# ReLU and row sum of 64 MiB on one core: row blocks laid out contiguously, and one store of short runs in place of one store of long runs

## The chip, the cores and the metric

The kernel runs on one core of one Trainium2 chip. The metric is the device time of an execution in microseconds (us). The span of a profile is mostly about 1.3 us shorter than that time.

## The reference

```python
x = np.random.randn(32, 512, 1024).astype(np.float32)     # 64 MiB
def reference(x):
    return np.sum(np.maximum(x, 0), axis=-1)               # (32, 512), 64 KiB
```

There are 16,384 rows of 4 KiB, and each gives one number.

## The kernel before

The rows are spread over 128 partitions, 128 rows for each. The first region gives every partition 112 consecutive rows. It is loaded in seven transfers of 16 rows per partition (8 MiB). The second region gives every partition 16 rows. It is loaded in ever smaller pieces (8, 4, 2, 1 rows, then the last row in three parts), so that little work is left after the last byte. All loads go through the SyncE queue, into three buffers.

```python
REGIONS = [112, 16]
CHUNKS = [(0, 0), (0, 16), (0, 32), (0, 48), (0, 64), (0, 80), (0, 96)]
...
xv = [xr[P * s : P * (s + n), :].rearrange("(p j) d -> p j d", p=P)
      for s, n in zip(start, REGIONS)]
ov = [of[P * s : P * (s + n)].rearrange("(p j) -> p j", p=P) ...]
...
for c in range(NBIG + 1):
    if c >= NB:
        sp.wait_ge(s_dve, done[c - NB])          # the buffer is free again
    if c < NBIG:
        g, j = CHUNKS[c]
        sp.dma_start(out=buf[:, c % NB, :, :], in_=xv[g][:, j : j + BIG, :]).then_inc(s_in[c], 16)
...                                              # the pieces of the last region
sp.wait_ge(s_fact, 1); sp.wait_ge(s_fdve, 1)     # the seven blocks are reduced
for g in range(len(REGIONS) - 1):                # runs once: 128 runs of 112 x 4 = 448 B
    sp.dma_start(out=ov[g][:, :], in_=res[:, start[g] : start[g] + REGIONS[g]]).then_inc(s_store, 16)
...                                              # ScalarE and VectorE work
sp.wait_ge(s_tdve, 1)                            # the last row is reduced
sp.dma_start(out=ov[-1][:, :], in_=res[:, start[-1] : J]).then_inc(s_out, 16)
sp.wait_ge(s_store, 16 * (len(REGIONS) - 1))
sp.wait_ge(s_out, 16)
```

In six of the blocks ScalarE applies ReLU and VectorE sums the rows. The other rows are done whole by one engine or the other. The change does not touch this.

Of the kernel before, what the change touches and what calls it, by code (L numbers as in the profile page):

```python
# [3 lines left out]
P = 128  # L4
D = 1024
BIG = 16
NB = 3
REGIONS = [112, 16]
CHUNKS = [(0, 0), (0, 16), (0, 32), (0, 48), (0, 64), (0, 80), (0, 96)]
ACT_STEPS = [[7, 9], [7, 9], [4, 5, 7], [4, 5, 7], [4, 5, 7], [3, 4, 5]]  # L10
DVE_STEPS = [[7, 9], [7, 4, 5], [4, 5, 7], [4, 5, 7], [4, 5, 7], [3, 4, 5]]
TAIL = [8, 4, 2, 1]
LAST = [512, 256, 256]


def bass_relu_sum_kernel(
# [15 lines left out]

    B, S, _ = x.shape
    J = B * S // P
    NBIG = len(CHUNKS)
    assert BIG * NBIG + sum(TAIL) + 1 == J == sum(REGIONS) and sum(LAST) == D

    xr = x.rearrange("b s d -> (b s) d")
    of = out.rearrange("b s -> (b s)")
    start = [sum(REGIONS[:i]) for i in range(len(REGIONS))]  # L40
    xv = [
        xr[P * s : P * (s + n), :].rearrange("(p j) d -> p j d", p=P)
        for s, n in zip(start, REGIONS)
    ]
    ov = [of[P * s : P * (s + n)].rearrange("(p j) -> p j", p=P) for s, n in zip(start, REGIONS)]

    buf = nc.alloc_sbuf_tensor("buf", [P, NB, BIG, D], fp32)
    last = nc.alloc_sbuf_tensor("last", [P, LAST[2] + 2], fp32)
    half = nc.alloc_sbuf_tensor("half", [P, 2], fp32)
    res = nc.alloc_sbuf_tensor("res", [P, J], fp32)  # L50

    n_in = NBIG + len(TAIL) + len(LAST)
    s_in = [nc.alloc_semaphore(f"s_in{i}") for i in range(n_in)]
# [7 lines left out]
    s_store = nc.alloc_semaphore("s_store")  # L61
    s_out = nc.alloc_semaphore("s_out")

    sp, act, dve = nc.sync, nc.scalar, nc.vector
# [4 lines left out]

    tb = NBIG % NB  # L70

# [6 lines left out]
    )  # L78
    for c in range(NBIG + 1):
        if c >= NB:  # L80
            sp.wait_ge(s_dve, done[c - NB])
        if c < NBIG:
            g, j = CHUNKS[c]
            sp.dma_start(out=buf[:, c % NB, :, :], in_=xv[g][:, j : j + BIG, :]).then_inc(
                s_in[c], 16
            )
        if c == 0:
            code.insert(arrival, code.pop())
    r = 0
    tail = []  # L90
    for i, n in enumerate(TAIL):
        sp.dma_start(out=buf[:, tb, r : r + n, :], in_=xv[-1][:, r : r + n, :]).then_inc(  # L92
            s_in[NBIG + i], 16
        )
# [7 lines left out]
        )  # L102
    sp.wait_ge(s_fact, 1)
    sp.wait_ge(s_fdve, 1)
    for g in range(len(REGIONS) - 1):
        sp.dma_start(
            out=ov[g][:, :], in_=res[:, start[g] : start[g] + REGIONS[g]]
        ).then_inc(s_store, 16)


    def on_act(t, acc):
# [11 lines left out]
    for c in range(NTWO):  # L123
# [17 lines left out]
        for n in DVE_STEPS[c]:  # L141
            if ready[r + n - 1] > seen:
# [3 lines left out]
                out=res[:, c * BIG + r : c * BIG + r + n],  # L146
                in_=buf[:, c % NB, r : r + n, :],
# [14 lines left out]
    for r, n, s in tail[:-1]:  # L162
# [6 lines left out]
    r, _, s = tail[-1]  # L169
# [6 lines left out]
        out=res[:, j0 + r : j0 + r + 1], in0=half[:, 0:1], in1=half[:, 1:2], op=ALU.add  # L176
    )

    n = LAST[2]
# [7 lines left out]


    sp.wait_ge(s_tdve, 1)
    sp.dma_start(out=ov[-1][:, :], in_=res[:, start[-1] : J]).then_inc(s_out, 16)  # L190
    sp.wait_ge(s_store, 16 * (len(REGIONS) - 1))
    sp.wait_ge(s_out, 16)


# [26 lines left out]
```

## Time and profile before

| | before |
|---|---|
| time, median | 161.12 us (161.08 to 161.19, 3 runs) |
| span of the profile | 159.8 us |
| DMA queue occupied | 98.0% |
| a block of 8 MiB lands every | 19.35 us |
| large store: issue to landing | 10.7 us, at 157.96 us |
| small store: issue to landing | 1.4 us, at 159.7 us |

The rows are in the prediction below. For a kernel that waits for data, the instructions that open each block are a clock: their starts mark the landings, and their differences are the service times of the DMA engines.

### The profile page before, as it was taken

The numbers are of one execution on the slowest core, as the hardware profiler recorded it, in microseconds if no ns is written. First come the engines' busy times: TensorE is split into PE (matmuls) and PEld (weight loads), VectorE is DVE, ScalarE is ACT, GpSimd is POOL, SyncE is SP. The second block draws the span as 40 slices with busy tenths as digits, with TensorE's granted clock in tenths as the row PEclk, the third lists the DMA queues.
The fourth block names the chain that finished last, engine by engine and source line by source line (L and its number), as shares of the span: only waits on it lengthen the run. The fifth ranks groups of instructions, "written<-read, shape, count | busy, mean of one in ns | idle before, by whom it ended". The sixth has DMA issues, their size and how long they took to land.

```text
span 159.8 us, 148 instructions
## 1 busy us (share of the span) xinstructions
DVE 121.4 (76%) x58; ACT 101.5 (63%) x55; POOL 0.2 (0%) x4
## 2 busy tenths in 40 slices
DVE  0000000999959999999969989699899999598995
ACT  3000059990699808996099951999339980496974
POOL 0000000000000000000000000000000000000000
DMA  7996996996997998989969969969969969899994
GB/s 262 525 525 262 525 525 262 525 525 262 525 443 344 525 410 377 525 361 427 525 295 492 525 279 509 525 262 525 525 262 525 525 262 525 353 435 394 406 393 138
DMA packets 2305, 67.18 MB, mean 420 GB/s; under 512 B 512, under 2 KB 768, under 8 KB 1024
## 3 DMA queue, kind: packets, MB, share of 16 engines
q1 hardware_dynamic: 2304, 67.18, 98.0%
q14 instruction: 1, 0.01, 0.0%
HBM read 67.11 MB, written 0.07 MB: 420 GB/s over the span
## 4 chain that ended last, share of the span: by engine, by line
DMA 68%; ACT 18%; DVE 11%; SPq 1%; issue 0%
DMA buf<-in_x_dram 68%; ACT buf L130 18%; DVE res L145 11%; SPq L92 1%; SPq L100 0%; DVE buf L115 0%; DVE last L115 0%
## 5 line engine op out<-in xcount | busy, mean ns | idle before, releaser
L145 DVE TENSOR_REDUCE res<-buf 128x7 f32<-128x7168 f32 (+4 forms) x17 | 100.1, 5923 | 34.0 <-ACT buf L130 34.0
L130 ACT ACTIVATE buf<-buf 128x7168 f32<-128x7168 f32 (+4 forms) x16 | 80.7, 5099 | 46.5 <-DMA buf<-in_x_dram 46.5
L112 ACT ACTIVATE buf<-buf 128x1024 f32<-128x1024 f32 (+1 forms) x19 | 19.0, 1000 | 9.0 <-DMA buf<-in_x_dram 8.9
L115 DVE TENSOR_SCALAR_CACHE_REDUCE buf<-buf 128x1024 f32<-128x1024 f32 (+2 forms) x19 | 20.9, 1146 | 2.8 <-DMA buf<-in_x_dram 2.5
L112 ACT ACTIVATION_READ_ACCUMULATOR buf<-buf 128x1 f32 x19 | 3.5, 186 | 0.0
L130 ACT ACT_TABLE_LOAD x1 | 1.3, 1283 | 0.8 <-PEq L206 0.8
L115 DVE DVE_READ_ACCUMULATOR buf<-buf 128x1 f32 x19 | 1.6, 83 | 0.0
L115 DVE TENSOR_SCALAR_CACHE_REDUCE last<-last 128x258 f32<-128x258 f32 x1 | 0.4, 422 | 0.0
L175 DVE TENSOR_TENSOR res<-half 128x1 f32<-128x1 f32 x1 | 0.2, 160 | 0.1
L206 POOL MEMSET const-bfloat16-1.0<- 128x1 bf16 x1 | 0.1, 101 | 0.0
L206 POOL MEMSET const-uint8-127<- 128x1 uint8 x1 | 0.1, 101 | 0.0
L206 POOL MEMSET const-float32-0.0<- 128x1 f32 x1 | 0.1, 98 | 0.2 <-issue 0.2
L206 POOL MEMSET const-float32-1.0<- 128x1 f32 x1 | 0.1, 98 | 0.0
L115 DVE DVE_READ_ACCUMULATOR last<-last 128x1 f32 x1 | 0.1, 81 | 0.0
## 6 DMA issues: line engine op xcount, KB each, us to landing
buf<-in_x_dram SPq DMA_DIRECT2D x1, 4096.0 KB, 26.7
buf<-in_x_dram SPq DMA_DIRECT2D x1, 2048.0 KB, 31.2
buf<-in_x_dram SPq DMA_DIRECT2D x1, 1024.0 KB, 33.2
buf<-in_x_dram SPq DMA_DIRECT2D x1, 512.0 KB, 34.0
buf<-in_x_dram SPq DMA_DIRECT2D x1, 256.0 KB, 34.2
buf<-in_x_dram SPq DMA_DIRECT2D x1, 128.0 KB, 34.1
last<-in_x_dram SPq DMA_DIRECT2D x1, 128.0 KB, 34.0
buf<-in_x_dram SPq DMA_DIRECT2D x7, 36.3
```

The lines of the kernel that those rows point to most:

```text
L92: sp.dma_start(out=buf[:, tb, r : r + n, :], in_=xv[-1][:, r : r + n, :]).then_inc(s_in[NBIG + i], 16)
L112: return act.activation(t, t, AF.Relu, accum_out=acc)
L115: return dve.tensor_scalar(out=t, in0=t, scalar1=0.0, scalar2=None, op0=ALU.max, op1=ALU.add, accum_out=acc)
L130: act.activation(t, t, AF.Relu).then_inc(s_act, 1)
L145: dve.tensor_reduce(out=res[:, c * BIG + r : c * BIG + r + n], in_=buf[:, c % NB, r : r + n, :], axis=X, op=ALU.add,).then_inc(s_dve, 1)
L175: dve.tensor_tensor(out=res[:, j0 + r : j0 + r + 1], in0=half[:, 0:1], in1=half[:, 1:2], op=ALU.add)
L206: nc = _bacc.Bacc("TRN2", target_bir_lowering=False, num_devices=1)
```

## The change

Each of the seven blocks becomes 2,048 consecutive rows, contiguous in memory. A partition's 16 rows then stand 64 KiB after its neighbour's, where they stood 448 KiB apart. The loads become simpler in form. In return, the results of a partition for the seven blocks lie 8 KiB apart in the output, so one store writes 896 runs of 64 B in place of 128 runs of 448 B.

```diff
-REGIONS = [112, 16]
-CHUNKS = [(0, 0), (0, 16), (0, 32), (0, 48), (0, 64), (0, 80), (0, 96)]
+NREG = 8
...
+    xr = x.rearrange("b s d -> (b s) d").rearrange("(g p j) d -> g p j d", g=NREG, p=P)
+    xv = [xr[g] for g in range(NREG)]
+    bulk = of[0 : P * BIG * NBIG].rearrange("(g p j) -> p g j", p=P, j=BIG)
+    tail_out = of[P * BIG * NBIG :].rearrange("(p j) -> p j", p=P)
...
-            g, j = CHUNKS[c]
-            sp.dma_start(out=buf[:, c % NB, :, :], in_=xv[g][:, j : j + BIG, :]).then_inc(s_in[c], 16)
+            sp.dma_start(out=buf[:, c % NB, :, :], in_=xv[c][:, :, :]).then_inc(s_in[c], 16)
...
-    for g in range(len(REGIONS) - 1):
-        sp.dma_start(out=ov[g][:, :], in_=res[:, start[g] : start[g] + REGIONS[g]]).then_inc(s_store, 16)
+    sp.dma_start(
+        out=bulk, in_=res[:, 0 : BIG * NBIG].rearrange("p (g j) -> p g j", j=BIG)
+    ).then_inc(s_store, 16)
...
-    sp.dma_start(out=ov[-1][:, :], in_=res[:, start[-1] : J]).then_inc(s_out, 16)
-    sp.wait_ge(s_store, 16 * (len(REGIONS) - 1))
+    sp.dma_start(out=tail_out, in_=res[:, BIG * NBIG : J]).then_inc(s_out, 16)
+    sp.wait_ge(s_store, 16)
```

More of the change, by code (lines that the diff above doesn't have):

```diff
@@ L34, in bass_relu_sum_kernel @@
     J = B * S // P
-    NBIG = len(CHUNKS)
-    assert BIG * NBIG + sum(TAIL) + 1 == J == sum(REGIONS) and sum(LAST) == D
-    xr = x.rearrange("b s d -> (b s) d")
+    NBIG = NREG - 1
+    assert BIG * NBIG + sum(TAIL) + 1 == J == BIG * NREG and sum(LAST) == D
+    xr = x.rearrange("b s d -> (b s) d").rearrange("(g p j) d -> g p j d", g=NREG, p=P)
     of = out.rearrange("b s -> (b s)")
-    start = [sum(REGIONS[:i]) for i in range(len(REGIONS))]
-    xv = [
-        xr[P * s : P * (s + n), :].rearrange("(p j) d -> p j d", p=P)
-        for s, n in zip(start, REGIONS)
-    ]
-    ov = [of[P * s : P * (s + n)].rearrange("(p j) -> p j", p=P) for s, n in zip(start, REGIONS)]
+    xv = [xr[g] for g in range(NREG)]
+    bulk = of[0 : P * BIG * NBIG].rearrange("(g p j) -> p g j", p=P, j=BIG)
+    tail_out = of[P * BIG * NBIG :].rearrange("(p j) -> p j", p=P)
     buf = nc.alloc_sbuf_tensor("buf", [P, NB, BIG, D], fp32)
@@ L82, in bass_relu_sum_kernel @@
         if c < NBIG:
-            g, j = CHUNKS[c]
-            sp.dma_start(out=buf[:, c % NB, :, :], in_=xv[g][:, j : j + BIG, :]).then_inc(
-                s_in[c], 16
-            )
+            sp.dma_start(out=buf[:, c % NB, :, :], in_=xv[c][:, :, :]).then_inc(s_in[c], 16)
         if c == 0:
@@ L104, in bass_relu_sum_kernel @@
     sp.wait_ge(s_fdve, 1)
-    for g in range(len(REGIONS) - 1):
-        sp.dma_start(
-            out=ov[g][:, :], in_=res[:, start[g] : start[g] + REGIONS[g]]
-        ).then_inc(s_store, 16)
+    sp.dma_start(
+        out=bulk, in_=res[:, 0 : BIG * NBIG].rearrange("p (g j) -> p g j", j=BIG)
+    ).then_inc(s_store, 16)
     def on_act(t, acc):
```

## The prediction

> **What bounds the kernel now.** I read the page first: its busy shares, the DMA rows and the chain that ended last.
>
> ```profile
> span 159.8 us, 148 instructions
> DVE 121.4 (76%) x58; ACT 101.5 (63%) x55; POOL 0.2 (0%) x4
> ...
> DMA packets 2305, 67.18 MB, mean 420 GB/s; under 512 B 512, under 2 KB 768, under 8 KB 1024
> ...
> q1 hardware_dynamic: 2304, 67.18, 98.0%
> ...
> DMA 68%; ACT 18%; DVE 11%; SPq 1%; issue 0%
> ```
>
> The reader is to see that no compute engine is near full, while the one DMA queue keeps its 16 engines occupied for 98.0% of the span. The ACT and DVE pieces of the chain are only times at which a buffer had to come free before the next load could be queued. Loads were queued far ahead (36.3 us from issue to landing at the median, against some 19 us of service), so those waits starved nothing. The next view, the timeline, gives the service time: the first ScalarE instruction on each block starts when that block has landed.
>
> ```profile
> 60.55 14.04 ACT L130 ACTIVATE buf<-buf 128x4096 f32<-128x4096 f32 x3 [5.40 <-DMA buf<-in_x_dram]
> 79.89 14.04 ACT L130 ACTIVATE buf<-buf 128x4096 f32<-128x4096 f32 x3 [5.30 <-DMA buf<-in_x_dram]
> 99.25 14.04 ACT L130 ACTIVATE buf<-buf 128x4096 f32<-128x4096 f32 x3 [5.32 <-DMA buf<-in_x_dram]
> ...
> 137.96 1.06 ACT L112 ACTIVATE buf<-buf 128x1024 f32<-128x1024 f32 x1 [6.65 <-DMA buf<-in_x_dram]
> ...
> 147.66 1.06 ACT L112 ACTIVATE buf<-buf 128x1024 f32<-128x1024 f32 x1 [1.28 <-DMA buf<-in_x_dram]
> ```
>
> Starts step by 19.34 and 19.36 us per block of 8 MiB; 8,388,608 B / 19.35 us = 433.5 GB/s. From 137.96 to 147.66, 9.70 us, the 4 MiB piece of the last region lands: 432.4 GB/s. ScalarE idles over 5 us ahead of every block, so arithmetic is hidden.
>
> Then the end, which the change also touches: the DMA queue's own waits, the issues on the page, and the timeline of the two stores.
>
> ```profile
> SPq L190 <- DVE last L115: 10.7, 1, 10.7
> SPq L192 <- DMA out_dram<-res: 1.1, 1, 1.1
> ```
>
> ```profile
> out_dram<-res SPq DMA_DIRECT2D x1, 56.0 KB, 10.7
> out_dram<-res SPq DMA_DIRECT2D x1, 8.0 KB, 1.4
> ```
>
> ```profile
> 147.26 0.35 SPq L106 DMA_DIRECT2D out_dram<-res  x1
> ...
> 158.33 0.34 SPq L190 DMA_DIRECT2D out_dram<-res  x1
> ```
>
> The 56 KB store is issued at 147.26 and lands at 147.26 + 10.7 = 157.96: it stands in the queue behind the last loads. Line 190 waits for the last reduction, until 158.33, so the small store lands at 158.33 + 1.4 = 159.7, the end of the span. The final wait for stores is 1.1 us, and it is the small store that it waits for.
>
> **What the Trainium skill says.** All four places are on the page "DMA: Bandwidth & Descriptors". Section "Where 436 GB/s comes from": 16 ports of 32 bytes at 850 MHz make 435.2 GB/s. The trace agrees: 433.5 GB/s is 99.6% of it, so a load can hardly become faster whatever its layout. Section "Specifications": a transfer needs at least 512 B for line rate, and below that the engine does read-modify-write. Both stores are below it already (448 B and 64 B runs), and their cost is read from the trace below. Section "Measured": about 10.5 ns per packet for the smallest transfers. The trace's 64-byte store gives nearly the same figure (below). Section "Latency and other measured facts": copies with a row pitch of 512 KiB per partition ran at 207 GB/s per direction and of 4 MiB at 103, where a full rate was 214; contiguous tiles are advised. Before, the pitch between partitions is 112 rows x 4 KiB = 448 KiB, not a power of two; the trace shows full rate. After it is 64 KiB.
>
> **The change part by part.** (1) Removed: the seven loads from a region with 448 KiB between partitions. Added: seven loads of one contiguous 8 MiB block each, 64 KiB per partition. Bytes, destination, run length (16 rows x 4 KiB = 64 KiB) and number of transfers are the same. The last region, with the tail loads and the last row's three pieces, has the same addresses as before: it is rows 14,336 to 16,383 in both. The service time of a block rests on the port ceiling, and the last region has shown the new 64 KiB pitch already, at 432.4 against 433.5 GB/s; the difference of 0.25% is about the fixed cost of twice the packets per byte. So 7 x 19.35 us stays 7 x 19.35 us: 0.0 us, and I allow 0.2 either way.
>
> (2) Start. The first block lands at 21.84 us, 2.49 later than one service time. A view of the queue in the window 1 to 4 us shows why in part:
>
> ```profile
> DMA packets 16, 1.05 MB, mean 350 GB/s; under 512 B 0, under 2 KB 0, under 8 KB 0
> ## 3 DMA queue, kind: packets, MB, share of 16 engines
> q1 hardware_dynamic: 16, 1.05, 103.1%
> ```
>
> Sixteen first packets of 64 KiB took 1.031 x 3 us x 16 engines / 16 = 3.09 us each, against about 2.42 in the steady state (64 KiB at 433.5/16 GB/s per engine). That 0.67 us is all that a better locality of the first accesses could bring back. I see no reason that it comes from the pitch, and count 0.1 us of gain.
>
> (3) Removed: one store of 128 runs of 448 B. Added: one store of 128 x 7 = 896 runs of 64 B (16 results of 4 B), because a partition's results now belong to seven blocks 8 KiB apart in the output. On 16 engines that is 56 packets each for 8. The price of a 64-byte packet, from the queue in the window 159.1 to 159.4 us, which holds the small store alone:
>
> ```profile
> DMA packets 144, 0.01 MB, mean 28 GB/s; under 512 B 144, under 2 KB 144, under 8 KB 144
> ## 3 DMA queue, kind: packets, MB, share of 16 engines
> q1 hardware_dynamic: 144, 0.01, 30.7%
> ```
>
> 0.307 x 0.3 us x 16 / 144 = 10.2 ns a packet (128 of 64 B and 16 that raise the semaphore). The same working on the window 157.27 to 157.5, with mostly 448-byte packets (38 packets, 21.9%), gives 0.219 x 0.23 x 16 / 38 = 21.2 ns. So an engine needs 56 x 10.2 = 0.57 us for the new store where it needed 8 x 21.2 = 0.17: +0.40 us. These packets follow the last loads in the queue, so no load is delayed by them; the landing moves from 157.96 to about 158.4. The small store goes out at 158.33 anyway and its first packets appear near 159.17, as the first filled slices of its window show. The 56 KB store's packets ended by 157.5. The slack is 159.17 - 157.5 = 1.7 us, over four times the 0.4. On the path: 0.0 us.
>
> (4) One store and one semaphore target in place of a loop that ran once: the same instruction count, 0. DVE and ACT work is identical.
>
> Sum: 0.0 - 0.1 + 0.0 = -0.1 us, and I round to no change: 161.1 us.
>
> **The rivals.** First, the power-of-two pitch makes the 16 engines collide in memory. If the skill's 512 KiB ratio applied (207/214, 3.3% slower), the seven blocks' 135 us would grow by 4.5 us, to 165.6. For it speaks that engines now run in step at multiples of 64 KiB; against it, the last region did so at full rate. Second, 64-byte writes in numbers cost more than a short burst of eight shows, as read-modify-writes back up in memory. At four times the price, 41 ns, the store takes 56 x 41 = 2.3 us, 2.1 more than before; 1.7 are hidden and the end moves by 0.4, to 161.5. At ten times it would be 5.7 us and some 165. The trace has no long series of such writes, so this is the step that I know least. Third, contiguous blocks are read better at the start: at most 0.67 us, 160.4. Fourth, a fully contiguous source might be cut into other packets than 64 KiB. The small store, contiguous in memory as a whole, still went in 128 packets of 64 B, which speaks against it; smaller load packets of 4 KiB or more would cost a few per mille.
>
> **Range and chances.** Three runs of before lie within 0.11 us. The third rival and the hidden part of the second bound the likely outcomes: 160.6 to 161.7 should hold it 8 times in 10. Within 2% means 157.9 to 164.3. Faster would need the port ceiling to be broken: 1%. Slower needs the first rival in nearly full strength or the second at over eight times the price: 3%. Within 2%: 96%.
>
> **What would show it.** Step 1: blocks again land 19.3 to 19.4 us apart. Step 2: the first ScalarE instruction near 21.8 us, not below 21.1. Step 3: 2305 + 768 = 3073 packets, 512 + 768 = 1280 under 512 B; the 56 KB store lands 10.9 to 11.3 us after issue; the final wait of the queue is still for the small store and stays near 1.1 us. The prediction is wrong if blocks land over 19.7 us apart, or if the large store lands after about 159.2 us and holds the small one back.

## The result, and the profile after

The changed kernel took 161.64 us (median of 6 runs, 161.34 to 161.82), against 161.14 of before in the same rounds (161.08 to 161.23). The ratio is 1.0029, with a 95% interval of 1.0016 to 1.0042. Ratios here are the mean time of one kernel's runs over the mean of the other's of the same rounds, so not quite the ratio of the medians. Executions over 1.5% slower than the fastest of the same kernel are left out of the means. The time lies within the predicted range, the change is "within 2%", and yet the 0.5 us is clear of the noise.

The page after shows the packets as forecast, 3073 in all:

```profile
span 160.5 us, 148 instructions
...
DMA packets 3073, 67.18 MB, mean 419 GB/s; under 512 B 1280, under 2 KB 1536, under 8 KB 1792
...
q1 hardware_dynamic: 3072, 67.18, 98.2%
```

The span grew by 0.7 us in this execution, which was one of the two slowest of the six (161.82). The timeline of ScalarE, in the lines where a block has landed, shows where that comes from (start, duration, instruction; in brackets the idle time before it and what ended it):

```profile
60.52 14.04 ACT L122 ACTIVATE buf<-buf 128x4096 f32<-128x4096 f32 x3 [5.40 <-DMA buf<-in_x_dram]
79.92 14.04 ACT L122 ACTIVATE buf<-buf 128x4096 f32<-128x4096 f32 x3 [5.36 <-DMA buf<-in_x_dram]
99.52 14.04 ACT L122 ACTIVATE buf<-buf 128x4096 f32<-128x4096 f32 x3 [5.56 <-DMA buf<-in_x_dram]
119.00 10.63 ACT L122 ACTIVATE buf<-buf 128x3072 f32<-128x3072 f32 x3 [5.44 <-DMA buf<-in_x_dram]
138.57 1.06 ACT L104 ACTIVATE buf<-buf 128x1024 f32<-128x1024 f32 x1 [6.86 <-DMA buf<-in_x_dram]
...
148.28 1.06 ACT L104 ACTIVATE buf<-buf 128x1024 f32<-128x1024 f32 x1 [1.29 <-DMA buf<-in_x_dram]
```

The start of the third block, 60.52, is where it was before (60.55). Then the steps are 19.40, 19.60, 19.48 and 19.57 us where they were 19.34 to 19.36. The seventh block starts at 138.57 and not at 137.96, 0.61 us later. The 4 MiB piece after it takes 9.71 us again. So nearly the whole growth lies in the loads of blocks four to seven. The records of single packets show it at the smallest scale. Before, a 64 KiB packet takes 2.418 us almost always, once the first packet of each engine is through. In the changed kernel's fifth block the first four packets of the 16 engines together take 4.3 us more than that, or 0.27 us per engine, and the last four nothing more. In the sixth and seventh blocks it is again the first packets that are slow.

The end of the kernel moved along with it. These are the issues of the two stores, and the queue's last waits:

```profile
out_dram<-res SPq DMA_DIRECT2D x1, 56.0 KB, 11.1
out_dram<-res SPq DMA_DIRECT2D x1, 8.0 KB, 1.4
```

```profile
SPq L182 <- DVE last L107: 10.7, 1, 10.7
SPq L184 <- DMA out_dram<-res: 1.1, 1, 1.1
```

The large store lands 11.1 us after its issue instead of 10.7, and the last wait is 1.1 us as before: it is still for the small store. By the trace's landings the large store is complete at 158.96 us and the small one at 160.41, 1.45 us later.

### The profile page after: what moved, and what is told of

Its sections match the earlier page's. It is cut to its first block, busy times and chain, and to the rows that moved or that the text cites. A ratio compares the mean times of both kernels' runs of the same rounds, so it can differ in the third digit from the quotient of the medians.

```text
span 160.5 us, 148 instructions
## 1 busy us (share of the span) xinstructions
DVE 121.4 (76%) x58; ACT 101.4 (63%) x55; POOL 0.2 (0%) x4
## 2 busy tenths in 40 slices
DMA packets 3073, 67.18 MB, mean 419 GB/s; under 512 B 1280, under 2 KB 1536, under 8 KB 1792
## 3 DMA queue, kind: packets, MB, share of 16 engines
q1 hardware_dynamic: 3072, 67.18, 98.2%
## 4 chain that ended last, share of the span: by engine, by line
DMA 68%; ACT 17%; DVE 11%; SPq 1%; issue 0%; DVEq 0%
DMA buf<-in_x_dram 68%; ACT buf L122 17%; DVE res L137 11%; SPq L85 1%; SPq L93 0%; DVE last L107 0%; DVE buf L107 0%; DVEq L177 0%
```

## The experiments

There were two theories to begin with. L says that the loads with 64 KiB between partitions cost the 0.5 us. S says that it is the store. Twelve kernels were run, four on each of three chips, each set against before on the same chip. Those whose results stand in the wrong places on purpose are named.

### The changed kernel again, and each half of the change alone

The first is the changed kernel without an edit.

> The changed kernel unedited, as the yardstick on this chip. Theory L (the loads: with 64 KiB between partitions single load packets take longer from the fourth block interval on) and theory S (the store of 64-byte runs) both expect 161.3 to 161.8 us against 161.1 of before. If the 0.5 us was a matter of the chip or of the moment alone, it comes out at 161.1. In the profile, L expects the intervals between landings of blocks 4, 5, 6 and 7 to be 19.45 to 19.6 us again, not 19.35.

Measured: 161.50 us (161.18 to 161.99), ratio 1.0027 (1.0012 to 1.0042). The loss repeats on another chip. In its profile, of the execution at 161.99, the slow blocks were other ones:

```profile
79.95 14.04 ACT L122 ACTIVATE buf<-buf 128x4096 f32<-128x4096 f32 x3 [5.30 <-DMA buf<-in_x_dram]
99.31 14.04 ACT L122 ACTIVATE buf<-buf 128x4096 f32<-128x4096 f32 x3 [5.32 <-DMA buf<-in_x_dram]
119.05 10.63 ACT L122 ACTIVATE buf<-buf 128x3072 f32<-128x3072 f32 x3 [5.70 <-DMA buf<-in_x_dram]
138.72 1.06 ACT L104 ACTIVATE buf<-buf 128x1024 f32<-128x1024 f32 x1 [6.96 <-DMA buf<-in_x_dram]
```

The steps are 19.36, 19.74 and 19.67: the fifth block is clean here, and the sixth and seventh are worse. My expectation that blocks four to seven would be slow again is half missed.

Next, the new loads with the old store (wrong places):

```diff
-        out=bulk, in_=res[:, 0 : BIG * NBIG].rearrange("p (g j) -> p g j", j=BIG)
+        out=of[0 : P * BIG * NBIG].rearrange("(p j) -> p j", p=P), in_=res[:, 0 : BIG * NBIG]
```

> The changed kernel's loads with a store of 128 runs of 448 B (results in the wrong places, on purpose). L expects the time of the changed kernel, 161.3 to 161.8 us. S expects that of before, 161.1 us.

Measured: 161.57 us (161.05 to 161.60, five runs), ratio 1.0024 (1.0011 to 1.0037). L holds. One of its five runs took 161.05 us, and the profile is of that one:

```profile
99.18 14.04 ACT L122 ACTIVATE buf<-buf 128x4096 f32<-128x4096 f32 x3 [5.31 <-DMA buf<-in_x_dram]
118.53 10.63 ACT L122 ACTIVATE buf<-buf 128x3072 f32<-128x3072 f32 x3 [5.31 <-DMA buf<-in_x_dram]
137.88 1.06 ACT L104 ACTIVATE buf<-buf 128x1024 f32<-128x1024 f32 x1 [6.65 <-DMA buf<-in_x_dram]
```

With the block before at 79.83, the steps are 19.35 throughout. The same loads can thus run as fast as before.

Then the old loads with the new store (wrong places):

```diff
+    bulk = of[0 : P * BIG * NBIG].rearrange("(g p j) -> p g j", p=P, j=BIG)
-    for g in range(len(REGIONS) - 1):
-        sp.dma_start(out=ov[g][:, :], in_=res[:, start[g] : start[g] + REGIONS[g]]).then_inc(s_store, 16)
+    sp.dma_start(out=bulk, in_=res[:, 0 : BIG * NBIG].rearrange("p (g j) -> p g j", j=BIG)).then_inc(s_store, 16)
```

> The loads of before with the store of 896 runs of 64 B (results in the wrong places, on purpose). L expects 161.1 us, as before, with the store landing some 11.1 us after its issue and the last wait still about 1.1 us. S expects 161.3 to 161.8 us.

Measured: 161.16 us (161.15 to 161.47), ratio 1.0005 (0.9993 to 1.0017). The store landed 11.0 us after its issue, and the last wait was 1.1 us. S falls as the cause of the whole loss: the store alone is not to be told from no change. The interval leaves room for at most 0.17%, some 0.3 us.

### Is it the addresses, or the time in the run?

The blocks in reverse order (wrong places):

```diff
-in_=xv[c][:, :, :]
+in_=xv[NBIG - 1 - c][:, :, :]
```

> The changed kernel with its seven blocks loaded in the reverse order (results in the wrong places, on purpose). If the slow packets belong to the addresses of blocks 4 to 6, the slow intervals move to the front: blocks landing first to third come at about 19.5 us and the later ones at 19.35. If they belong to the time in the run, or to how far the engines have drifted apart, intervals 4 to 6 stay slow at 19.5 to 19.6. Total 161.3 to 161.8 us either way.

Measured: 161.69 us (161.21 to 161.95), ratio 1.0031 (1.0018 to 1.0044). The profile's blocks, third to seventh in time:

```profile
60.56 14.04 ACT L122 ACTIVATE buf<-buf 128x4096 f32<-128x4096 f32 x3 [5.39 <-DMA buf<-in_x_dram]
80.20 14.04 ACT L122 ACTIVATE buf<-buf 128x4096 f32<-128x4096 f32 x3 [5.61 <-DMA buf<-in_x_dram]
99.71 14.04 ACT L122 ACTIVATE buf<-buf 128x4096 f32<-128x4096 f32 x3 [5.46 <-DMA buf<-in_x_dram]
119.20 10.63 ACT L122 ACTIVATE buf<-buf 128x3072 f32<-128x3072 f32 x3 [5.45 <-DMA buf<-in_x_dram]
138.58 1.06 ACT L104 ACTIVATE buf<-buf 128x1024 f32<-128x1024 f32 x1 [6.67 <-DMA buf<-in_x_dram]
```

The steps are 19.64, 19.51, 19.49 and 19.38. The slow stretch did not move to the front, as fixed addresses would have had it. It begins at the fourth landing and fades at the seventh. Neither forecast fits wholly: the stretch belongs neither to given blocks nor to given positions. What the slow profiles share is that they start clean, that some two to four consecutive blocks are then slow, and that the place differs. The packet records add two things. Within a stretch the same packet of an engine's eight tends to be the slow one in block after block: the first in the changed kernel's profile (0.09, 0.09 and 0.13 us more per engine in blocks five to seven), the fifth here (0.13, 0.09 and 0.13 in blocks four to six). And how nearly the 16 engines are in step does not tell a slow execution from a clean one: the fourth block's first packets start within 0.55, 0.59 and 0.46 us of one another in the three slow profiles, and within 0.52 us in the clean one (new loads, old store).

### How far apart must the partitions be?

The distance in memory between the data of neighbouring partitions is called the pitch below. These four go back to the code of before and change only the two lists of regions and blocks (the edit of the second list is left out here), with correct results. Each has one profile, of one execution. The first two mix wide and contiguous blocks.

```diff
-REGIONS = [112, 16]
+REGIONS = [64, 16, 16, 16, 16]        # blocks 1-4 at 256 KiB, 5-7 at 64 KiB
```

> First four blocks from a region with 256 KiB between partitions, last three contiguous (64 KiB), a store per region; right results. The runs so far show that the slow intervals come in executions at changing places (third to sixth), and in one execution not at all. If 64 KiB between partitions in a late block makes its packets slow, some of the intervals 5 to 7 are over 19.45 us in most executions and the time is 161.2 to 161.7. If what counts is how the first blocks were laid out (engines brought out of step by them), it is 161.1.

Measured: 161.44 us (161.29 to 161.59) against 161.19, ratio 1.0015 (1.0003 to 1.0028). The time fits the first reading, but the profile, of a run at 161.29, shows no slow block (steps of 19.35 to 19.36 for the last three). Its first block starts late instead, at 22.06 us. Undecided.

```diff
-REGIONS = [112, 16]
+REGIONS = [16, 16, 16, 16, 48, 16]    # blocks 1-4 at 64 KiB, 5-7 at 192 KiB
```

> First four blocks contiguous (64 KiB), last three from a region with 192 KiB between partitions, five small stores and one of the tail; right results. If 64 KiB in the late blocks is what is slow, the intervals 5 to 7 go back to 19.35 us and the time is 161.1, at most 161.3. If the early blocks leave the engines in a bad state, the late intervals stay at 19.5 and the time at 161.3 to 161.8.

Measured: 161.33 us (161.24 to 161.50), ratio 1.0010 (0.9996 to 1.0023). The steps of the last three are 19.34, 19.36 and 19.38 us. In this execution the early contiguous blocks left nothing behind that the late wide ones suffer from; but they were clean themselves (steps of 19.32 to 19.36), so it proves little. A time of 161.3 is at the edge of what was expected.

```diff
-REGIONS = [112, 16]
+REGIONS = [48, 64, 16]                # blocks 1-3 at 192 KiB, 4-7 at 256 KiB
```

> Blocks 1 to 3 with 192 KiB between partitions, blocks 4 to 7 with 256 KiB; right results. If any power of two between partitions is slow in late blocks, 161.3 to 161.8 us with intervals over 19.45 among the last four. If it is the 64 KiB (a block contiguous in memory) that matters, 161.1.

Measured: 161.18 us (161.07 to 161.29), ratio 0.9998 (0.9986 to 1.0011), all steps 19.31 to 19.36. Here 256 KiB, a power of two, costs nothing measurable in late blocks.

```diff
-REGIONS = [112, 16]
+REGIONS = [64, 48, 16]                # blocks 1-4 at 256 KiB, 5-7 at 192 KiB
```

> Blocks 1 to 4 with 256 KiB between partitions, blocks 5 to 7 with 192 KiB; right results. 161.1 us under both readings of the pitch (a power of two only in the early blocks, which showed no slow interval before the third so far); over 161.3 would mean that any pitch below 448 KiB is slow.

Measured: 161.31 us (161.28 to 161.41), ratio 1.0009 (0.9996 to 1.0022). No step is slow; in the profile the first block starts at 22.04 us, where it was 21.84 before (on another chip), and that makes up the 0.2 us of that execution. The other kernel that begins with 256 KiB started late too (22.06); two profiles are too few to call it the pitch.

The last one of this kind:

```diff
-REGIONS = [112, 16]
+REGIONS = [32, 32, 32, 16, 16]        # blocks 1-6 at 128 KiB, 7 at 64 KiB
```

> All but the last full block from regions with 128 KiB between partitions (32, 32, 32, then 16 and 16 rows per partition), right results. If it takes just 64 KiB to make late blocks slow, 161.1 to 161.3 and all intervals 19.35 (the last full block may be up to 19.45). If 128 KiB does it too, 161.3 to 161.8 and some interval from the third on over 19.45.

Measured: 161.35 us (161.32 to 161.57) against 161.23, ratio 1.0012 (1.0000 to 1.0025). All steps of the blocks lie between 19.34 and 19.36, the last one too. The profile has a delay at one small piece near the end instead, which started 156.64 us where it was 156.34 before. So 128 KiB shows no slow block either; a remainder of about 0.1% in the time is at the edge of the noise and not explained.

### Does it help to bring the engines out of step?

An extra load for eight of the engines at the start, from another queue, added to the changed kernel:

```diff
+    act.dma_start(
+        out=extra[:, :], in_=xr[0, 0:8, 0:3, :].rearrange("p j d -> p (j d)")
+    ).then_inc(s_extra, 16)
```

> The changed kernel with one extra load of 8 partitions x 12 KiB from the ScalarE queue at the start, which should occupy eight of the 16 engines for some 0.45 us and so spread their position within a block wider than now; right results. The engines that carry it end 0.45 us later, so 161.5 to 161.6 us if all intervals become 19.35 (the slow stretches come from engines in near step), and 161.8 to 162.2 with intervals over 19.45 if being in step has nothing to do with it.

Measured: 163.18 us (162.97 to 163.65), ratio 1.0127. This is outside both forecasts, because the means was unfit. In the window 6.3 to 9.9 us, the packets of all 16 engines became slower, not of eight:

```profile
DMA packets 24, 1.15 MB, mean 319 GB/s; under 512 B 0, under 2 KB 0, under 8 KB 0
## 3 DMA queue, kind: packets, MB, share of 16 engines
q1 hardware_dynamic: 16, 1.05, 94.7%
q10 hardware_dynamic: 8, 0.10, 8.9%
```

The 16 packets of the large load took 0.947 x 3.6 us = 3.41 us on average in place of 2.42. The first block was started on at 23.48 us, 1.6 later than before. After that all steps are 19.34 to 19.36. One profile without a slow stretch proves little, since the changed loads had one such run as well. This experiment is inconclusive.

### What does a short run in a store cost?

The prediction was least sure here. The loads of before are kept, so that no slow stretch disturbs, and the large store is cut finer (wrong places). This is the code for runs of 16 B; for 8 B the 4 becomes 2.

```diff
+    src = res[:, 0 : BIG * NBIG].rearrange("p (g j) -> p g j", j=BIG)
+    for j in range(0, BIG, 4):
+        sp.dma_start(out=bulk[:, :, j : j + 4], in_=src[:, :, j : j + 4]).then_inc(s_store, 16)
```

> The loads of before, the large store cut into four stores of 896 runs of 16 B (results in the wrong places, on purpose). The store of 64-byte runs landed 11.0 us after issue against 10.7 of 448-byte runs: 0.3 us for 48 more packets per engine, 6.2 ns each. 224 packets per engine are 216 more than before: 1.35 us at 6.2 ns, 2.1 us at the 10.2 ns that I took from the small store. If the cost lies in the slack of 1.7 us at the lower price, the time is 161.1 to 161.2. At the higher price it is 161.5. If packets are dearer in numbers, it is over 162.

Measured: 164.30 us (164.02 to 164.41) against 161.23, ratio 1.0189 (1.0175 to 1.0203). The third forecast is right: packets in numbers are dearer. In the queue's waits:

```profile
SPq L192 <- DMA out_dram<-res: 4.3, 1, 4.3
SPq L190 <- DVE last L115: 0.7, 1, 0.7
```

The last wait is 4.3 us in place of 1.1, and the span ends at 163.0. But in the window 159.5 to 163.1 us no data packet is left:

```profile
DMA packets 1, 0.01 MB, mean 2 GB/s; under 512 B 0, under 2 KB 0, under 8 KB 0
## 3 DMA queue, kind: packets, MB, share of 16 engines
q14 instruction: 1, 0.01, 2.4%
```

The last data packet ends at 159.41, and the small store is reported as landed at 158.36 + 4.6 = 162.96, some 3.6 us later. Before, this gap was 0.4 us (159.38 and 159.76). The cost of these short writes is not in the packet times that I had taken it from. It is in the landing. Not only the number of packets changed, though: the runs are shorter, there are four stores, and each writes a quarter of the same 64 B. Which of these makes the landing late was not tested.

> The same with eight stores of 896 runs of 8 B: 448 packets per engine, 440 more than before. At 6.2 ns they take 2.7 us more, 1.0 more than the slack: about 162.1 us. At 10.2 ns they take 4.5 us, 2.8 past the slack: 163.9. If small packets cost nothing that the end sees, 161.1. The large store's packets would then stand ahead of the small store's, and the last wait grows from 1.1 us by the same amount.

Measured: 169.86 us (169.42 to 170.00), ratio 1.0529 (1.0512 to 1.0545). All three forecasts are far too low. From 224 to 448 packets per engine the medians grow by 169.86 - 164.30 = 5.56 us, 24.8 ns per packet. Issuing costs too: the eight issues occupied the queue's sequencer for 13.82 us, so that the small store went out at 161.38, 3 us late. The 24.8 ns is therefore a price for the whole, not for the write alone. Here the packets themselves became slow as well. In the window 159.5 to 163 us:

```profile
DMA packets 2642, 0.03 MB, mean 8 GB/s; under 512 B 2641, under 2 KB 2641, under 8 KB 2641
q1 hardware_dynamic: 2641, 0.02, 185.8%
```

That is 1.858 x 3.5 us x 16 / 2641 = 39 ns a packet; a share over 100% means that records overlap. The last packet ended at 165.37 and the last landing came 3.2 us after it.

The store of 64-byte runs is far from this: in the changed kernel it landed 1.45 us ahead of the small store, so it stayed hidden.

## Why the prediction was right or wrong

**The bound.** Right. The queue is full (98.2%), the VectorE and ScalarE work is the same (121.4 and 101.4 us), and nothing in the arithmetic moved.

**Step 1, the loads: the term that was mis-sized.** The prediction put it at 0.0 us, with 0.2 either way, on the ground that the last region had shown the 64 KiB pitch at full rate. It measured about 0.5: the ratio is 1.0024 with the new loads alone (some 0.4 us), and 0.61 us in the profiled execution. Its own sign, blocks 19.3 to 19.4 us apart, was missed with steps up to 19.60, and its sign of being wrong, over 19.7, was reached once (19.74 in the repeated run). The evidence was true but too short: one piece of 4 MiB, 9.7 us, in one execution, and in packets of 32 KiB where the blocks' are of 64 KiB. The slow stretches appear in some executions only, and in the profiles here not before the third full interval. So a cost of up to 0.9 us in one execution and 0.0 in another could not be seen in it. The first rival named the right part of the kernel, the loads with this pitch. Its size of 3.3%, an estimate from the figure for 512 KiB of the Trainium skill ("DMA: Bandwidth & Descriptors", "Latency and other measured facts"), was ten times too large, and its reason (powers of two) is not borne out at 256 KiB: late blocks gave 0.9998. What sets a stretch off, and why it ends, is not settled. That the engines collide in memory is not shown by any run.

**Step 2, the start.** Right within its size: 0.1 us of gain was counted, and the first block started at 21.81 us against 21.84.

**Step 3, the store.** Right in its outcome, and right by the margin more than by the price. It was to land 10.9 to 11.3 us after its issue, and it took 11.1; it was to stay hidden, and alone it measures 1.0005. The price of 10.2 ns came from packet records and fits this store (its packets took 11 ns); with 224 to 448 packets per engine the whole costs 24.8 ns for each further one. The slack of 1.7 us was taken from packet records as well; by landings it is 1.45 us. The second rival, that short writes in numbers cost more, is borne out in its outcome and does not bite at 56 packets per engine. That they back up as read-modify-writes is not shown.

**Step 4 and the fourth rival.** Right: 148 instructions as before, 64 KiB load packets, 3073 packets in all. The rival's size was misread: in the trace of before a 4 KiB packet of the tail took 159 ns, so 64 KiB in such packets would take 2.54 us in place of 2.42, 5% and not a few per mille.

The sum of -0.1 us should have been about +0.5. Still 161.64 falls within 160.6 to 161.7, near its upper end. That is owed to the width of the range and not to step 1: the range was drawn for a late store and an early start, and for the loads 0.2 us were allowed.

## What to carry to other kernels

When loads keep the DMA queue full as here (98.0%), a new layout has little to win, so ask what it may lose; here rows that stand closer together brought slow stretches in some executions, and a region with 112 rows per partition, which also stores its results in longer runs, stayed the best layout, level with [48, 64, 16]. A short clean stretch of a profile does not prove a layout for a whole run: look at several executions, block by block. Judge a store of many short runs by its landing and by the last wait, not by the packet durations of a few short ones; it is free only while its landing stays ahead of another one that ends the kernel.

## What the Trainium skill lacked or had wrong

- "DMA: Bandwidth & Descriptors", section "Latency and other measured facts", gives pitches from 512 KiB up for copies and advises contiguous tiles. It has nothing on smaller ones. Here loads of contiguous 8 MiB tiles (64 KiB pitch) were the slower ones, by 0.24 to 0.31% in four kernels, while 192 and then 256 KiB was level with 448 KiB (0.9998).
- The same page, section "Measured", gives 10.5 ns per packet of the smallest transfers, for loads issued by GpSimd. The trace agrees for the packet durations of a small store (10.2 ns). What the page lacks is a price for a store of many short runs: the time grew by 24.8 ns for each further packet per engine between 224 and 448 (delayed issues included), and landings came up to 3.6 us after the last packet's record, against 0.4 us before.
- The same page, section "Issuing engines are not separate DMA queues", calls the time to initiate a DMA usually small relative to the DMA itself. Stores of many short runs behind queued loads held the sequencer for 10.38 us (four issues) and 13.82 us (eight), where one of them took 9.8 and 7.4 us at the median from issue to landing.
- No page that I read says that a small load from a second queue slows more than its own engines. Here, while 96 KB for eight partitions were loaded in eight packets, one 64 KiB packet on each of the 16 engines took 1.0 us more on average (3.41 in place of 2.42 us), in the one execution profiled.
